# Two modulation tiles moved from a feed-forward's middle to beside the output projection ahead of it, and a rounding of value weights moved behind an exponential

## The chip, the core and the metric

The kernel runs on one core of a Trainium2 chip. The metric is the device time of one execution in microseconds. Before the change the median of three runs is 1470.91 us (1470.82 to 1471.57). One more execution was taken by the hardware profiler; it took 1470.03 us, and its trace, all of whose times count from the first instruction, spans 1468.2 us. Engine names: PE is TensorE (matmuls), DVE is VectorE, ACT is ScalarE, POOL is GpSimd, SP is the engine that issues most of the DMAs. Every engine works through its own instructions in order.

## The reference: what is computed

One step of a two-layer diffusion backbone for 128 context and 512 latent tokens of 1024 features:

```python
    for l in range(DEPTH):
        sh1_p, sc1_p, g1_p, sh2_p, sc2_p, g2_p = ada_modulation(cond_ctx, w_mod[l], b_mod[l])
        sh1_s, sc1_s, g1_s, sh2_s, sc2_s, g2_s = ada_modulation(cond_lat, w_mod[l], b_mod[l])
        hp = modulate(rms_norm(xp, norm_mix[l]), sh1_p, sc1_p)
        hs = modulate(rms_norm(xs, norm_mix[l]), sh1_s, sc1_s)
...
        xp = xp + g1_p * out_p
        xs = xs + g1_s * out_s
        hp = modulate(rms_norm(xp, norm_ffn[l]), sh2_p, sc2_p)
        hs = modulate(rms_norm(xs, norm_ffn[l]), sh2_s, sc2_s)
        xp = xp + g2_p * swiglu(hp, w_ffn_in[l], w_ffn_out[l])
        xs = xs + g2_s * swiglu(hs, w_ffn_in[l], w_ffn_out[l])
```

`ada_modulation` is silu(condition) @ w_mod + b_mod, 6 x 1024 numbers for each layer and condition. The mixer of layer 0 has 8 latent-attention (MLA) heads and 8 neighbourhood heads, that of layer 1 grouped-query attention. The feed-forward has 2816 hidden columns.

## The kernel before, in words

All 640 tokens stand along the free axis, the features along the 128 partitions. A float32 product is made of three matmuls of rounded parts (`mm3`: high x high, high x low, low x high). So each weight tile that comes from memory is split: ACT copies it to the rounded type (the high part, L175, L1490, L1025) and DVE subtracts that from the raw tile (the low part, L176, L1491, L1026).

**Modulation.** The sum over 1024 inputs for 128 modulation columns is one tile (`wm`, 128 x 1024 floats, 512 KB). For layer 0 part of it is made by PE (`mod0`: matmuls, a copy `modsb` by ACT at L373, a second small matmul, the bias by DVE at L381). The rest (layer 0's last gate, tiles 40 to 47 of `mods[0]`, and layer 1) is made by DVE: `one` (in `mod_side`) loads a tile and multiplies it with the broadcast conditions, once for each of the two conditions, summing as it goes (L1750, output `junk`). `mod_side` holds one list of 48 tiles in order and two functions that take from its front: `before` takes tiles beside an output projection (loads of L1768 into two buffers `ws`), as many after each of the 8 column blocks as a tuple says; `start` takes them inside the feed-forward, as many as `plan(kind, i)` says, for `kind` "fb" after hidden block i, for "n" in the feed-forward's output part.

**Neighbourhood heads** (layer 0) run from a written order of pieces for each head; the pieces of the values (`tail`) of one head run within the next. Beside head 6 the value weights of MLA (`wmv`, two halves of 128 x 512) are loaded and split at L1025 and L1026, well ahead of their use. `nexps[h, j]` is the instruction of head h's exponential j (L804), and `after(inst, fn)` has `fn`'s instructions issued behind `inst`. Other names there: `nts` are transposed probabilities split at L405 (ACT) and L409 (DVE), `no` the values' products, `ns` scores, `L475` and `L420` sum two halves of an output on DVE.

**Output projection of layer 0** (`mixer_out`, names `oa`): 8 column blocks; for each, weights `oaw` are split, PE multiplies, DVE adds gate x product to the residual stream (L335), ACT squares it (L213, L208) and DVE sums the squares (L214). Blocks 5 to 7 do their first token half first; `oanp` then sums over partitions on PE, and from its result come the feed-forward's inputs `h01`.

**Feed-forward of layer 0** (`ffn(0, ...)`). From hidden block 3 on, each block of 128 hidden columns is made by seven products instead of eight (a Strassen-like scheme) whose weights `wX`, `wW`, `wY`, `wZ` come out of `seven`: DVE adds the raw gate weights `rg` (`wg_`) and up weights `ru` (`wu_`) at L1298, L1299, L1302 and L1303 (output `s`), and ACT and DVE split them. The raw gate weights go into two buffers (`wr`), loaded at L1611. Per block PE does `fg<-..11`, `fd<-..D`, the last product `E` of the block before, `fg<-..N`, `fu`, `fd<-..22`, and `fg<-..C`, which may write its bank only when ACT has copied `u` from it (L1624). After the block's `E`, DVE multiplies gate and up (`sg`, L1599), ACT and DVE split the result (`hd`, L1550, L1551), and SP writes it out (`sp_`, L1556). A scheduler then places these instructions on each engine, by its own estimate of when they can run. As it has placed them, DVE makes the sums `s` of block N while PE is at the products of block N - 2, and the tile that the plan gives to block N, both products of it, runs on DVE in that same stretch. I call the stretch in which `s` of block N is made round N.

Of the kernel before, what the change touches and what calls it, by code (L numbers as in the profile page):

```python
# [13 lines left out]
AF = mybir.ActivationFunctionType  # L14
# [37 lines left out]
def body(ctx, tc, xT, vecs, crow, wm0, wm0g1, wm0g, wm1, wA, wNV, wNA, wMK, wMV, wOA, wGQ, wGK, wGV, wOC,  # L52
# [3 lines left out]
    V, S, G = nc.vector, nc.scalar, nc.gpsimd  # L56
# [32 lines left out]
    def bank(name, kind="m"):  # L89
        if kind == "m":  # L90
            return psp.tile([P, 512], F32, tag="m", bufs=4, name=name)
        return ypool["pool"].tile([P, 512], F32, tag=kind, bufs=ypool["tags"][kind], name=name)
# [13 lines left out]
    def f(ap):  # L106
        return ap.bitcast(F32)
# [13 lines left out]
    def sequence(order, pieces):  # L121

        left = dict(pieces)
        run([left.pop(name) for name in order.split() if name in left])
        assert not left, list(left)

    def named(prefix, pieces):
        return {f"{prefix}{i}": piece for i, piece in enumerate(pieces)}
# [17 lines left out]
    mods = [main.tile([P, 48, 2], F32, name=f"mods{l}") for l in range(2)]  # L146
# [32 lines left out]
    def after(inst, fn):  # L179
        if inst is None:  # L180
            return fn()
        with tc.issue_after(inst.ins):
            return fn()
# [340 lines left out]
    x = []  # L524
# [182 lines left out]
    nqk, wnas, done_with, nexps = {}, {}, {}, {}  # L707
# [242 lines left out]
    mqs, exps = {}, {}  # L950
# [24 lines left out]
    for h in range(8):  # L975
        p, r = divmod(h, 2)
        if r == 0:
            oN.append(ring.tile([P, T], F32, tag="x", name=f"oN{p}"))
            pfirst, psecond = prompt_pair([nv[4][:, 2 * p + i, :] for i in range(2)], oN[p], ab, f"npp{p}",
                                         lambda name: bank(name, "y"))  # L980
        pts = []
        sc = na_scores(h, bm, pts)
        if h < 7:
            bm = na_bias(h + 1)
        qh, ql, ks = [t[r] for t in nqk[p]]
        pieces = named("s", sc)
        if h in SPLIT_AT:
            pieces["pk"] = lambda h=h: after(nexps[h, 1], SPLIT_AT[h])

        def prompt_scores(pss, qh=qh, ql=ql, ks=ks):  # L990
            PE.matmul(pss, qh[:, NS:T], ks[:, 896:1024], start=True, stop=False)
            PE.matmul(pss, ql[:, NS:T], ks[:, 896:1024], start=False, stop=True)
        pieces["sp"] = pfirst(r, prompt_scores)
        if p < 3:
            pieces.update(named("q", na_q(p + 1) if r == 0 else na_k(p + 1)))
        for n, at in enumerate(M_AT):
            if h == at:
                pieces.update(named("n" if "m0" in pieces else "m", mod0(4 + n, lambda n=n: bank(f"mod{4 + n}", "y"),
                                                                               mod_raw_w if h == 6 else mod_raw)))
        if h == 7:  # L1000
            pieces.update(k_pieces(0, ybank))
            pieces.update(named("u", q_pieces(0, ybank, lambda c: ring.tile([P, T], F32R, tag="h" + c, name=f"mq{c}0"),
                                              lambda: f(tq[0]))))
        sequence(NA_ORDER[h] if h else "q0 q1 s0 m0 q2 s1 sp pk q3 q4 q5 m1 q6 q7 m2", {**pieces, **tail})
        tail = na_values(h, pts, oN[p])
        if r == 1:
            tail.update(psecond)
        if h == 6:
            mla_w(0)
            kT = [[ring.tile([P, T], F32R, tag="h" + c, name=f"kT{c}{r}") for r in range(2)] for c in "hl"]  # L1010
            kTp = ring.tile([P, T], F32R, tag="x", name="kTp")
            even_keys, first_odd = [[(kT[i][r], kTp[:, P * (2 * i + r):P * (2 * i + r + 1)]) for i in range(2)] for r in range(2)]
            odd_keys = [first_odd]
            wmvr = [ring.tile([P, T], F32R, tag="hh", name=f"wmvr{u}") for u in range(2)]
            tq = [ring.tile([P, T], F32R, tag="hh", name=f"tq{r}") for r in range(2)]
            with tc.issue_after(fetched["wm0r"].ins):
                for u in range(2):
                    fetched["wmvr"] = nc.sync.dma_start(f(wmvr[u][:, :512]), wMV[:, 512 * u:512 * u + 512])
                lat = latents()
            with tc.issue_after(fetched["near"].ins):  # L1020
                fetched["tq"] = nc.sync.dma_start(f(tq[0]), tabM[:, 0, :])
            wmv = wp.tile([P, 2, 1024], F32R, tag="w", bufs=3, name="wmv")
            for u in range(2):
                c = slice(512 * u, 512 * u + 512)
                S.activation(wmv[:, 0, c], f(wmvr[u][:, :512]), AF.Copy)  # L1025
                V.tensor_tensor(wmv[:, 1, c], f(wmvr[u][:, :512]), f(wmv[:, 0, c]), ALU.subtract)  # L1026
            wmv = wmv[:, 0, :], wmv[:, 1, :]
        if h == 7:
            with tc.issue_after(fetched["tq"].ins):
                for r in range(2):  # L1030
                    k_rope(r, (slice(64, 128), slice(0, 64))[r])
                nc.sync.dma_start(f(tq[1]), tabM[:, 1, :])
# [83 lines left out]
    tail, oM, oNs = {}, [], []  # L1116
# [33 lines left out]
    oMs = [after(exps[7, 3], lambda: rsplit(oM[p], f"oMs{p}")) for p in range(3)]  # L1150
# [639 lines left out]
    def x_again(n):  # L1790
# [5 lines left out]
    op = ffn_open(0)  # L1796
    box, nxt = next_mod("h01", gs[0][1], mods[0], SH2, op[7])
    side, before = mod_side([(0, wm0g, G2)] + [(1, wm1[j:j + 8], j) for j in (SH1, SC1, G1, SH2, SC2)],
                            lambda kind, i: int(4 < i < 20 and (i % 3 > 0 or i in (9, 15))) if kind == "fb" else
                            (0, 1, 1, 1, 2, 2, 2, 2, 3, 3, 3, 3, 3, 2, 2, 2)[i])  # L1800
    x, pend = mixer_out(wOA, oMs + oNs, [4, 5, 6, 7, 0, 1, 2, 3], x_again, mods[0], "oa", nxt, op[-1], before(op[1], op[5], (1, 1, 1, 1, 0, 0, 0)), True, hold=exps[7, 3])
    box2, nxt = next_mod("h10", gs[1][0], mods[1], SH1)
    x, pend = ffn(0, x, pend, box["m"], nxt, side, op)

# [187 lines left out]
    for h in range(8):  # L1992
# [4 lines left out]
        if h < 7:  # L1997
# [10 lines left out]
    op = ffn_open(1)  # L2008
    box, nxt = next_mod("h11", gs[1][1], mods[1], SH2, op[7])
    _, before = mod_side([(1, wm1[G2:], G2)], None)  # L2010
    x, pend = mixer_out(wOC, oGs, list(range(8)), lambda n, x=x: x[n], mods[1], "oc", nxt, op[-1],
                        before(op[5], op[5], (2, 1, 1, 2, 1, 1, 0)), True, hold=gexp[7, 3])
# [11 lines left out]
    x, pend = ffn(1, x, pend, box["m"], final, lambda pool: lambda kind, i: None, op)  # L2024
# [158 lines left out]
```

## Time and profile before

| What | us |
|---|---|
| median of 3 runs | 1470.91 |
| the profiled execution | 1470.03 |
| its span, first to last instruction | 1468.2 |
| neighbourhood head 6's end, where `wmv` is split | 187 to 202 |
| output projection `oa` of layer 0 | 311 to 369 |
| feed-forward of layer 0, seven-product blocks | 413 to 651 |
| its output part | 651 to 806 |
| product of a modulation tile and one condition on DVE (L1750) | 1.22 |
| load of a 512 KB tile `wm`, median from issue to landing | 4.4 |

A row of a timeline gives the start, the length, the engine, the line, the operation with its output and inputs, and in brackets how long the engine sat idle ahead of it and what ended that. Times of lists of waits are totals, counts and the longest.

### The profile page before, as it was taken

To read this page: it belongs to the slowest core of one execution; us is meant where nothing else is said; L and a number is where in the kernel's file an instruction comes from. 1 tells how busy PE (TensorE), PEld (TensorE's weight loads), DVE (VectorE), ACT (ScalarE), POOL (GpSimd) and SP (SyncE) were. 2 spreads that over 40 slices of the span, in tenths; PEclk is the share of its full clock that TensorE was granted. 3 is DMA by queue.
4 is the path that set the end of the run, shared out by engine and by line. 5 is a ranking of instruction groups with operands and counts; after the bars stand their busy time and mean duration, and the time that the engine had idled before them with its cause. 6 is when DMAs were issued, how large, how long until landed. Compare 5 with 4: busy or idle time off the path is not lost.

```text
span 1468.2 us, 25868 instructions
## 1 busy us (share of the span) xinstructions
PE 1435.2 (98%) x9764; PEld 1387.6 (95%) x9764; DVE 1230.0 (84%) x2353; ACT 776.6 (53%) x1531; POOL 179.4 (12%) x276
## 2 busy tenths in 40 slices
PE   5999999999999999999999999999999999999997
PEld 3989989899999999999999999989999999999997
DVE  5877778977998898856998888888899898989976
ACT  5446667853755454531223666672656555555443
POOL 0047635520000000000000122220000000000000
PEclk9999999999999999999999999999999999999999
DMA  9643460134265454468765200115245555548572
GB/s 370 223 155 125 145 188 17 44 136 138 89 214 179 159 167 156 161 231 319 228 224 158 98 30 30 57 50 170 84 167 196 178 181 178 178 141 293 185 268 72
DMA packets 82725, 234.18 MB, mean 160 GB/s; under 512 B 9256, under 2 KB 15560, under 8 KB 82216
## 3 DMA queue, kind: packets, MB, share of 16 engines
q1 hardware_dynamic: 80240, 228.12, 46.3%
q10 hardware_dynamic: 1944, 3.48, 0.7%
q8 instruction: 76, 1.25, 0.3%
q0 software_dynamic: 416, 0.93, 0.2%
q14 instruction: 49, 0.40, 0.1%
HBM read 192.82 MB, written 36.66 MB: 156 GB/s over the span
## 4 chain that ended last, share of the span: by engine, by line
PE 81%; DVE 9%; DMA 4%; ACT 3%; issue 2%; SPq 0%; DVEq 0%; ACTq 0%
PE fg L64 17%; PE fd L64 7%; PE fgo L64 5%; PE fo L64 5%; PE gq L64 3%; PE fu L64 3%; PE fdo L64 2%; PE nk L64 2%; PE go L64 2%; PE gs L64 2%; PE nq L64 1%; PE fuo L64 1%; PE gt L68 1%; DVE junk L1750 1%; PE mod L64 1%
## 5 line engine op out<-in xcount | busy, mean ns | idle before, releaser
L1750 DVE SCALAR_TENSOR_TENSOR junk<-wm,cb 128x1024 bf16<-128x1024 f32 x88 | 107.4, 1221 | 2.7 <-DMA wm<-in_wm 1.7
L64 PE MATMUL gq<-h10h,wgq 128*128 128x320 f32 x256 | 65.8, 316 | 0.0
L269 POOL TENSOR_SCALAR h10h<-h10t,gs,mods 128x320 fp32r<-128x320 f32 x4 | 3.9, 991 | 432.8 <-DVE h10t L263 426.8
L1490 ACT ACTIVATE wY<-s 128x1024 fp32r<-128x1024 f32 x38 | 40.3, 1061 | 23.3 <-PE fg L64 19.1
L2018 POOL TENSOR_TENSOR xr<-xw,fn1rs 128x320 f32<-128x320 f32 x2 | 1.7, 861 | 412.8 <-ACT fn1rs L237 412.8
L1599 DVE TENSOR_TENSOR sg<-up,sg 128x640 f32<-128x640 f32 x38 | 31.3, 824 | 21.5 <-ACT sg L1598 20.4
L1491 DVE TENSOR_TENSOR wZ<-s,wZ 128x1024 fp32r<-128x1024 f32 x38 | 46.4, 1220 | 1.3
L1490 ACT ACTIVATE wZ<-s 128x1024 fp32r<-128x1024 f32 x38 | 40.1, 1055 | 13.7 <-PE fd L64 9.0
L1491 DVE TENSOR_TENSOR wY<-s,wY 128x1024 fp32r<-128x1024 f32 x38 | 46.3, 1220 | 0.3
L64 PEld LDWEIGHTS gq<-h10h,wgq 128*128 128x128 f32 x256 | 44.9, 189 | 0.6
L1598 ACT ACTIVATE sg<-fg 128x320 f32<-128x320 f32 x38 | 16.7, 438 | 48.2 <-PE fg L64 48.2
L64 PE MATMUL fg<-h01C,wY 128*128 128x320 f32 x228 | 37.1, 311 | 2.7 <-ACT u L1624 2.7
L64 PE MATMUL gq<-h10l,wgq 128*128 128x320 f32 x128 | 39.4, 308 | 0.0
L1955 ACT ACTIVATE gp<-gs,gb,rq 128x640 f32<-128x640 f32 (+1 forms) x40 | 31.8, 796 | 13.2 <-DVE gb L1954 11.8
L1620 ACT ACTIVATE p<-fd 128x320 f32<-128x320 f32 x38 | 16.6, 437 | 40.7 <-PE fd L64 40.7
L64 PEld LDWEIGHTS fg<-h01C,wY 128*128 128x128 f32 x228 | 34.0, 188 | 4.2 <-ACT u L1624 4.2
L64 PE MATMUL fg<-h11N,wZ 128*128 128x320 f32 x228 | 36.7, 309 | 0.0
L64 PE MATMUL fg<-h01q,wX 128*128 128x320 f32 x228 | 36.7, 309 | 0.0
L64 PE MATMUL fu<-h11q,wX 128*128 128x320 f32 x228 | 36.6, 309 | 0.0
L64 PE MATMUL fg<-h01E,wW 128*128 128x320 f32 x228 | 36.6, 309 | 0.0
L64 PE MATMUL fg<-h01N,wZ 128*128 128x320 f32 x228 | 36.6, 309 | 0.0
L64 PE MATMUL fd<-h11q,wZ 128*128 128x320 f32 x228 | 36.6, 309 | 0.0
(3412 smaller groups left out, 5287.0 us busy)
## 6 DMA issues: line engine op xcount, KB each, us to landing
wm<-in_wm SPq DMA_DIRECT2D x48, 512.0 KB, 4.4
mraw<-in_wm SPq DMA_DIRECT2D x8, 1024.0 KB, 13.2
mraw<-in_wm SPq DMA_DIRECT2D x14, 512.0 KB, 3.8
wmv<-in_wm0g SPq DMA_DIRECT2D x8, 512.0 KB, 4.1
wm<-in_wm0g SPq DMA_DIRECT2D x8, 512.0 KB, 4.6
ruo<-in_wFO SPq DMA_DIRECT2D x8, 512.0 KB, 4.4
rgo<-in_wFO SPq DMA_DIRECT2D x8, 512.0 KB, 6.3
x<-in_xT SPq DMA_DIRECT2D x8, 320.0 KB, 5.7
```

The costliest lines, as they stand in the source:

```text
L64: cls.last = nc.tensor.matmul(*a, **k)
L68: cls.last = nc.tensor.transpose(*a, **k)
L269: G.tensor_scalar(h[:, c0:c1], t, self.gsl[:, k, 0:1], self.ml[:, self.sh + k, 0:1], ALU.mult, ALU.add)
L1490: S.activation(h, src, AF.Copy)
L1491: V.tensor_tensor(w_, src, f(h), ALU.subtract)
L1598: last = S.activation(sg[:, 0:HT], g[:, :HT], AF.Silu, scale=-1.0)
L1599: V.tensor_tensor(sg, up, sg, ALU.mult)
L1620: S.activation(p5, b5[:, :HT], AF.Copy)
L1750: V.scalar_tensor_tensor(junk, raw, 1.0, cb[:, c, :], ALU.mult, ALU.mult, accum_out=mods[l][:, j0 + i, c:c + 1])
L1955: gexp[h, j] = S.activation(dst, src, AF.Exp, bias=nb, scale=rq[:, j:j + 1], accum_out=ll[:, j:j + 1])
L2018: G.tensor_tensor(x[k][:, c0:c1], root[1][k], nrm.rs[:, c0:c1], ALU.mult)
```

## The change

Three edits. The tuple for the output projection of layer 0 gives six tiles instead of four (tiles 44 and 45 of `mods[0]`, after its blocks 5 and 6). The plan of the feed-forward no longer takes a tile at hidden blocks 9 and 15; every tile behind 45 is taken from the same list, so it comes at an earlier block than before; behind the blocks all is as it was. And the first half of `wmv`'s high part is issued behind the last exponential of head 6.

```diff
             for u in range(2):
                 c = slice(512 * u, 512 * u + 512)
-                S.activation(wmv[:, 0, c], f(wmvr[u][:, :512]), AF.Copy)
+                after(nexps[6, 3], lambda: S.activation(wmv[:, 0, c], f(wmvr[u][:, :512]), AF.Copy))
                 V.tensor_tensor(wmv[:, 1, c], f(wmvr[u][:, :512]), f(wmv[:, 0, c]), ALU.subtract)
...
     side, before = mod_side([(0, wm0g, G2)] + [(1, wm1[j:j + 8], j) for j in (SH1, SC1, G1, SH2, SC2)],
-                            lambda kind, i: int(4 < i < 20 and (i % 3 > 0 or i in (9, 15))) if kind == "fb" else
+                            lambda kind, i: int(4 < i < 20 and i % 3 > 0) if kind == "fb" else
                             (0, 1, 1, 1, 2, 2, 2, 2, 3, 3, 3, 3, 3, 2, 2, 2)[i])
-    x, pend = mixer_out(wOA, oMs + oNs, [4, 5, 6, 7, 0, 1, 2, 3], x_again, mods[0], "oa", nxt, op[-1], before(op[1], op[5], (1, 1, 1, 1, 0, 0, 0)), True, hold=exps[7, 3])
+    x, pend = mixer_out(wOA, oMs + oNs, [4, 5, 6, 7, 0, 1, 2, 3], x_again, mods[0], "oa", nxt, op[-1], before(op[1], op[5], (1, 1, 1, 1, 1, 1, 0)), True, hold=exps[7, 3])
```

What it moves. ACT at the end of head 6, as a difference of the two orders (`np` are head 6's exponentials, `modsb` the modulation's copy that PE waits for):

```order
 L175 ACTIVATE wm_2497<-wm0r 128x768
-L1025 ACTIVATE wmv<-wmvr_2505 128x512
 L405 ACTIVATE nts_2h<-nt_2_2436 128x512
 L804 ACTIVATE np_2_2408,nl_2350<-np_2_2408,nm_2349 128x384
 L804 ACTIVATE np_3_2414,nl_2350<-np_3_2414,nm_2349 128x384
 L373 ACTIVATE modsb_2466<-mod_2420 128x256
+L1025 ACTIVATE wmv<-wmvr_2505 128x512
 L448 ACTIVATE npp3p,npp3l_2450<-npp3s_2445,npp3m_2448 128x128
 L1025 ACTIVATE wmv<-wmvr_2506 128x512
```

The first copy moves behind two exponentials and `modsb`; the second stays. On DVE both bias additions of L381 then stand ahead of the second L1026, where one and then the other stood behind it.

DVE in the output projection, from the residual of block 4 on; before:

```order
L335 SCALAR_TENSOR_TENSOR xr_4534<-oa4a,mods_98,xr_4534 128x320
L176 TENSOR_TENSOR oaw_4610<-oaw6r,oaw_4610 128x1024
L214 TENSOR_TENSOR oanacc<-oanacc,oansq_4538 128x320
L335 SCALAR_TENSOR_TENSOR xr_4534<-oa4b,mods_98,xr_4534 128x192
L335 SCALAR_TENSOR_TENSOR xr_4534<-oa4b,mods_98,xr_4534 128x128
L176 TENSOR_TENSOR oaw_4648<-oaw7r,oaw_4648 128x1024
```

and after:

```order
L335 SCALAR_TENSOR_TENSOR xr_4534<-oa4a,mods_98,xr_4534 128x320
L1750 SCALAR_TENSOR_TENSOR junk_4577,mods_98<-wm_44_4575,cbo 128x1024
L214 TENSOR_TENSOR oanacc<-oanacc,oansq_4538 128x320
L1750 SCALAR_TENSOR_TENSOR junk_4579,mods_98<-wm_44_4575,cbo 128x1024
L335 SCALAR_TENSOR_TENSOR xr_4534<-oa4b,mods_98,xr_4534 128x192
L335 SCALAR_TENSOR_TENSOR xr_4534<-oa4b,mods_98,xr_4534 128x128
L176 TENSOR_TENSOR oaw_4616<-oaw6r,oaw_4616 128x1024
L214 TENSOR_TENSOR oanacc<-oanacc,oansq_4567 128x320
L1750 SCALAR_TENSOR_TENSOR junk_4621,mods_98<-wm_45_4619,cbo 128x1024
L176 TENSOR_TENSOR oaw_4660<-oaw7r,oaw_4660 128x1024
```

The rounding of the last two blocks' weights now stands behind products of tiles 44 and 45; the second product of 45 comes two rows further down, ahead of the feed-forward's first weights.

DVE in the feed-forward in round 9 (`sg_6` is the gated product of block 6); before:

```order
L1298 TENSOR_TENSOR s_9_6109<-wg_9r 128x512
L1491 TENSOR_TENSOR wY_8_5976<-s_8_5973,wY_8_5976 128x1024
L1299 TENSOR_TENSOR s_9_6109<-wu_9r,wg_9r 128x512
L1750 SCALAR_TENSOR_TENSOR junk_6314,mods_98<-wm_47_6312,cb 128x1024
L1302 TENSOR_TENSOR s_9_6115<-s_9_6109,wg_9r 128x512
L1750 SCALAR_TENSOR_TENSOR junk_6316,mods_98<-wm_47_6312,cb 128x1024
L1599 TENSOR_TENSOR sg_6_5723<-up_6_5722,sg_6_5723 128x640
```

and after:

```order
L1298 TENSOR_TENSOR s_9_6122<-wg_9r 128x512
L1491 TENSOR_TENSOR wY_8_5988<-s_8_5985,wY_8_5988 128x1024
L1299 TENSOR_TENSOR s_9_6122<-wu_9r,wg_9r 128x512
L1302 TENSOR_TENSOR s_9_6128<-s_9_6122,wg_9r 128x512
L1303 TENSOR_TENSOR s_9_6128<-s_9_6128,wu_9r 128x512
L1599 TENSOR_TENSOR sg_6_5735<-up_6_5734,sg_6_5735 128x640
```

The two products are gone from ahead of `sg`. On SP the load of the next gate weights (`wg_10r`) now stands ahead of the write of block 6's hidden tile instead of behind it. Round 15 changes in the same way.

## The prediction

> **What bounds the kernel now.** I read the page first, then PE's waits, then PE's own timeline, and last the engines that PE waits for. The page:
>
> ```profile
> span 1468.2 us, 25868 instructions
> PE 1435.2 (98%) x9764; PEld 1387.6 (95%) x9764; DVE 1230.0 (84%) x2353; ACT 776.6 (53%) x1531; POOL 179.4 (12%) x276
> ```
>
> TensorE (PE) is the bound, so a change on other engines can only win what PE loses in waits. In the list of PE's waits (total, times, longest) the largest beyond the start-up is this one:
>
> ```profile
> PE fg L64 <- ACT u L1624: 2.7, 5, 0.8
> ```
>
> It lies in the first feed-forward's middle. There PE runs seven products for each block of 128 hidden columns, and the seventh, `fg<-h01C`, must wait until ACT has copied the fifth's result out of the same bank (`u`). PE's timeline (start, length, what, idle time before it) has one such row in each round (round N: DVE prepares the weights of block N); for rounds 8 to 12, 15 to 17 and 19:
>
> ```profile
> 458.22 1.92 PE L64 MATMUL fg<-h01C,wY 128*128 128x320 f32 x12
> ...
> 470.92 2.02 PE L64 MATMUL fg<-h01C,wY 128*128 128x320 f32 x12 [0.23 <-ACT u L1624]
> ...
> 484.31 2.03 PE L64 MATMUL fg<-h01C,wY 128*128 128x320 f32 x12 [0.81 <-ACT u L1624]
> ...
> 497.67 2.03 PE L64 MATMUL fg<-h01C,wY 128*128 128x320 f32 x12 [0.78 <-ACT u L1624]
> ...
> 510.10 1.92 PE L64 MATMUL fg<-h01C,wY 128*128 128x320 f32 x12
> ...
> 547.03 1.92 PE L64 MATMUL fg<-h01C,wY 128*128 128x320 f32 x12
> ...
> 560.14 2.02 PE L64 MATMUL fg<-h01C,wY 128*128 128x320 f32 x12 [0.63 <-ACT u L1624]
> ...
> 572.93 2.03 PE L64 MATMUL fg<-h01C,wY 128*128 128x320 f32 x12 [0.22 <-ACT u L1624]
> ...
> 597.86 1.92 PE L64 MATMUL fg<-h01C,wY 128*128 128x320 f32 x12
> ```
>
> Undisturbed, a round takes (547.03 - 510.10) / 3 = 12.31 us. From round 8 to 19 there are 11 periods, 135.4 us at that pace, and they took 139.64: PE loses **4.2 us** here. The five idle times add up to only 2.67. I use the starts, because a row's end runs past the start of the next (12 matmuls are recorded as 1.92 long where they follow each other in a seventh of 12.31, 1.76), so each idle time is shown about 0.16 too short, and the smaller waits between rounds 17 and 19 aren't listed at all. The Trainium skill (Perfetto Trace Analysis, the section on the Tensor Engine's instruction) says that a matmul's end is computed, not observed, which agrees; by the idle times the sum below would be 1.5 us smaller.
>
> Why ACT is late: a loop between DVE, ACT, SP and DMA that is longer than PE's period. Rows of DVE, ACT and SP in round 9:
>
> ```profile
> 463.71 0.69 DVE L1298 TENSOR_TENSOR s<-wg_9r 128x512 f32<-128x512 f32 x1 [1.64 <-DMA wg_9r<-in_wFI]
> ...
> 466.05 1.22 DVE L1750 SCALAR_TENSOR_TENSOR junk<-wm,cb 128x1024 bf16<-128x1024 f32 x1
> ...
> 467.80 1.22 DVE L1750 SCALAR_TENSOR_TENSOR junk<-wm,cb 128x1024 bf16<-128x1024 f32 x1
> ...
> 468.94 0.82 DVE L1599 TENSOR_TENSOR sg<-up,sg 128x640 f32<-128x640 f32 x1
> 469.80 0.74 ACT L1550 ACTIVATE hd_0h<-sg 128x640 fp32r<-128x640 f32 x1 [3.39 <-DVE sg L1599]
> 470.94 0.43 SPq L1611 DMA_DIRECT2D wg_10r<-in_wFI  x1
> 477.10 0.69 DVE L1298 TENSOR_TENSOR s<-wg_10r 128x512 f32<-128x512 f32 x1 [1.84 <-DMA wg_10r<-in_wFI]
> ```
>
> `sg` is late because the two products of a modulation tile (`junk`) stand before it; the next weights are asked for behind `sg` (7.23 us after the loop began), and DVE then idles until they land. Round: 477.10 - 463.71 = 13.39, 1.08 over PE's 12.31. PE's `C` product of this round started 470.92 - 463.71 = 7.21 behind `s`. Round 12, without a tile:
>
> ```profile
> 503.58 0.69 DVE L1298 TENSOR_TENSOR s<-wg_12r 128x512 f32<-128x512 f32 x1 [1.66 <-DMA wg_12r<-in_wFI]
> 508.83 0.33 SPq L1611 DMA_DIRECT2D wg_13r<-in_wFI  x1
> 513.36 0.68 DVE L1298 TENSOR_TENSOR s<-wg_13r 128x512 f32<-128x512 f32 x1
> ```
>
> The weights are asked for after 5.25 us, DVE doesn't wait for them, and the round is 9.78. Five tiles in a row drive PE into waits; one round without a tile resets the loop.
>
> **The change, part by part.** *Tiles out of rounds 9 and 15.* The rounds with tiles become 7, 8 | 10, 11 | 13, 14 | 16, 17. Up to round 8 nothing differs in kind, and the `C` of round 8 shows no wait. Round 9 begins at 463.71 as before; without its two products (468.94 - 467.80 = 1.14 each) its `C` isn't waited for and starts at 458.22 + 12.31 = 470.53. Round 10's `s` comes at 463.71 + 9.78 = 473.5, or 3.26 behind the last `C` (513.36 - 510.10), 473.8, whichever is later. Its `C` could start at 473.8 + 7.21 = 481.0 and PE gets there at 482.84. Round 11: 473.8 + 13.39 + 7.21 = 494.4 against 495.15. Round 12 has no tile, and 13 and 14 start from a reset loop like 10 and 11, as do 16 and 17: 0.7 us is the smallest margin. Gain: all **4.2**. Its lower bound has the tile-free round as slow in its load as the others (wg_10r: 477.10 - 470.94 = 6.16 instead of 4.53, round 11.4). Three rounds are then 2 x 13.39 + 11.4 = 38.2 against PE's 36.9. The walk gives `C` starts 0.6, 0.2, 1.1, 0.2 and 1.1 us late in rounds 11, 13, 14, 16 and 17, 3.1 in all before rounding, and a gain of 1.1.
>
> *The same work beside the output projection.* Four products more on DVE, and two loads on SP: wm_44 ahead of oaw7r, wm_45 ahead of the feed-forward's first weights. PE waits nowhere in this stage. DVE between 343 and 358 us (busy), the landing times of all `wm` loads, and the rows that set the deadlines:
>
> ```profile
> 343.00:358.00 15.00, 9.40 (x15) 1.00 0.54 176
> DMA to landing us min/median/max: 3.3/4.4/7.2
> 335.12 1.22 DVE L1750 SCALAR_TENSOR_TENSOR junk<-wm,cbo 128x1024 bf16<-128x1024 f32 x1
> ...
> 343.29 0.54 DVE L335 SCALAR_TENSOR_TENSOR xr<-oa4a,mods,xr 128x320 f32<-128x320 f32 x1
> 343.75 1.21 DVE L176 TENSOR_TENSOR oaw<-oaw6r,oaw 128x1024 fp32r<-128x1024 f32 x1
> 344.89 0.48 DVE L214 TENSOR_TENSOR oanacc<-oanacc,oansq 128x320 f32<-128x320 f32 x1
> 346.77 0.68 DVE L335 SCALAR_TENSOR_TENSOR xr<-oa4b,mods,xr 128x192 f32<-128x192 f32 x2 [1.40 <-PE oa4b L64]
> ...
> 357.33 0.55 DVE L335 SCALAR_TENSOR_TENSOR xr<-oa,mods,xr 128x320 f32<-128x320 f32 x1 [1.89 <-PE oa L64]
> 350.09 0.31 PE L64 MATMUL oa6a<-oNs0h,oaw 128*128 128x320 f32 x1
> 359.77 0.70 PE L64 MATMUL oanp<-oanacc,ones 128*128 128x320 f32 x2
> ```
>
> 4 x 1.22 = 4.9 us go into 5.6 us of idle time, ahead of the last residual at 357.33, which waits for PE anyway; behind it 1.9 us remain until `oanp` needs the sums of squares. By the new order DVE starts wm_44's first product at 343.75, where rounding oaw6r's weights (`L176`) stood, and does that rounding behind the residual of 346.77: 346.77 + 0.68 + 1.21, near 348.7. PE wants them at 350.09. wm_44 can be asked for when wm_42's second product ends (336.3); with 7.2 us, the longest landing, it is there at 343.5. Cost: **0**.
>
> *The rounding of the value weights.* Rows of ACT, PE and DVE at the end of neighbourhood head 6:
>
> ```profile
> 192.89 0.63 ACT L1025 ACTIVATE wmv<-wmvr 128x512 fp32r<-128x512 f32 x1 [0.63 <-DMA wmvr<-in_wMV]
> 193.42 0.58 ACT L405 ACTIVATE nts_2h<-nt 128x512 fp32r<-128x512 f32 x1
> ...
> 195.10 0.37 ACT L373 ACTIVATE modsb<-mod 128x256 f32<-128x256 f32 x1
> 195.52 0.61 PE L64 MATMUL mod<-sel,modsb 128*128 128x4 f32 x4 [0.73 <-ACT modsb L373]
> 198.10 0.41 PE L64 MATMUL ns<-nk,nqh 128*128 128x384 f32 x1 [0.35 <-DVE mods L381]
> 201.54 0.50 PE L64 MATMUL no<-nts_0l,nv 128*128 128x512 f32 x1 [0.36 <-DVE nts_0l L409]
> 196.37 0.83 DVE L1026 TENSOR_TENSOR wmv<-wmvr,wmv 128x512 fp32r<-128x512 f32 x1 [0.36 <-DMA cq1l<-cqr]
> 197.20 0.57 DVE L475 TENSOR_TENSOR oN<-npp2o,npp2h 64x128 f32<-64x128 f32 x2
> ```
>
> With the first half's copy behind `modsb`, ACT no longer idles 0.63 for its load and the 0.53 of the copy is gone from ahead of `modsb`: it comes about 1 us earlier and the 0.73 goes. DVE's `L381` now stands ahead of the second `L1026`, so the 0.35 goes. What is late next is the third wait: DVE's chain `L475` to `L409` starts behind the second `L1026`, whose copy ACT ends about 0.4 earlier, and DVE saves the `L381` between. I put the chain 0.6 earlier; PE, 1.1 earlier before it, waits longer there. Gain: **0.6**. Ends: all three waits gone, 1.44; or the copy's 0.53 pushed onto the chain behind it, a loss.
>
> *Sum* against the profiled execution (1470.03, of which 1468.2 is span): 4.2 + 0 + 0.6 = 4.8, so 1465.2. The median of the runs is 0.88 above it: 1470.91 - 4.8 = **1466.1**.
>
> **The rivals.** A, *one empty round isn't enough*: the tile-free load takes as long as the rest. For it: wg_9r, wg_10r and wg_12r all landed too late for DVE (1.64, 1.84 and 1.66 idle), and round 12 was reached with PE 2.6 us behind its pace, which eased it. Against: in round 12, where the load was asked for without products ahead of it, it was hidden. Gain 1.1 + 0.6: 1469.2.
>
> B, *slower: wm_44 lands late*. DVE takes its work in order, so oaw6r's rounding stands behind wm_44's first product and the matmuls at 350.09 behind that. From that product's start to the rounding's end it is 1.22 + 0.48 + 1.22 + 0.68 + 1.21 = 4.8 us by the rows (at most, since DVE's rows overlap a little), so it decides from a start at 345.3, a landing of 9.0 us. PE then stops for each us more; slower by over 0.2% needs 4.8 + 2.9 = 7.7 more, a landing of nearly 17 us: 1473.8. Against it: the longest of these loads took 7.2. The Trainium skill (DMA: Bandwidth & Descriptors, section on queues, rings and completion order) has one queue's transfers consumed in ring order on each engine, which speaks for it; no run here shows that order.
>
> C, *nothing changes*: PE comes 4.8 earlier to the second half of the feed-forward and waits there for reloaded hidden tiles or weights instead: 1470.9. Against: PE shows no wait of 0.2 from 600 to 800 us, and those loads follow PE's own progress.
>
> The change does do what it says: both moves stand in the order.
>
> **How the numbers follow.** Forecast 0.65, A 0.20, B 0.05, C 0.10. Low end: all of 4.2 and 1.44 gone, 1465.3, less 0.3 for the runs' scatter: 1465.0. High end: 1.1 and nothing from the rounding, 1469.8; C and B lie outside. 0.2% is 2.9 us, about what can be told from no change here. Faster: the forecast and a part of A, 0.68; same: the rest of A and C, and a little of the forecast, 0.26; slower 0.06.
>
> **What would show it.** In the changed profile: `fg<-h01C` rows 12.31 apart from round 8 to 19 with no idle time; no PE wait in 343 to 372 us; wg_10r and wg_16r asked for about 5.3 behind their `s`; `modsb` not waited for, and a longer wait at `nts_0l`. Wrong if those rows still wait in rounds 11, 14 or 17 (A), if `oa6a` or `oanp` waits (B), or if they run smoothly and new waits appear behind 600 us (C).

## The result, and the profile after

The changed kernel takes 1466.43 us (median of 7 runs, 1465.12 to 1469.15) against 1471.29 (7 runs of before beside it): ratio 0.9967, 95% interval 0.9955 to 0.9979. That is 4.86 us faster, 3.1 to 6.6 by the interval. The forecast was 4.8, to 1466.1. Its profiled execution took 1467.04, with a span of 1465.3 (before: 1470.03 and 1468.2), so the two traces differ by only 2.9; the parts below add up to that and say what belongs to the change.

PE's timeline of the changed kernel at the seventh products of rounds 8 to 11, 16 and 19:

```profile
458.57 1.92 PE L64 MATMUL fg<-h01C,wY 128*128 128x320 f32 x12
470.88 1.92 PE L64 MATMUL fg<-h01C,wY 128*128 128x320 f32 x12
483.20 1.92 PE L64 MATMUL fg<-h01C,wY 128*128 128x320 f32 x12
495.50 1.92 PE L64 MATMUL fg<-h01C,wY 128*128 128x320 f32 x12
...
557.08 1.92 PE L64 MATMUL fg<-h01C,wY 128*128 128x320 f32 x12
...
594.01 1.92 PE L64 MATMUL fg<-h01C,wY 128*128 128x320 f32 x12
```

No row carries an idle time, and the eleven periods take 594.01 - 458.57 = 135.44 instead of 139.64: 4.20 less, every wait gone. The loop behind it, in rows of DVE and SP:

```profile
463.83 0.69 DVE L1298 TENSOR_TENSOR s<-wg_9r 128x512 f32<-128x512 f32 x1 [1.97 <-DMA wg_9r<-in_wFI]
469.08 0.33 SPq L1611 DMA_DIRECT2D wg_10r<-in_wFI  x1
474.03 0.69 DVE L1298 TENSOR_TENSOR s<-wg_10r 128x512 f32<-128x512 f32 x1 [0.24 <-DVE g L1630]
...
487.18 0.69 DVE L1298 TENSOR_TENSOR s<-wg_11r 128x512 f32<-128x512 f32 x1 [1.06 <-DMA wg_11r<-in_wFI]
500.80 0.69 DVE L1298 TENSOR_TENSOR s<-wg_12r 128x512 f32<-128x512 f32 x1 [2.15 <-DMA wg_12r<-in_wFI]
```

Round 9, now without a tile, asks for the next weights 469.08 - 463.83 = 5.25 us behind its beginning, and DVE finds them there when it comes. The rounds take 10.20, 13.15 and 13.62: 36.97 for three, where PE needs 36.93. The next two groups of three take 36.17 and 36.52 (`s` of blocks 15 and 18 starts at 536.97 and 573.49). So the loop is about as long as PE's period, with little over; the experiments show what that means.

At the end of neighbourhood head 6 (rows of ACT and PE of the changed kernel):

```profile
193.43 1.07 PE L64 MATMUL mod<-mraww,scol 128*32 128x256 f32 x16
195.05 0.37 ACT L373 ACTIVATE modsb<-mod 128x256 f32<-128x256 f32 x1
195.61 0.56 PE L64 MATMUL mod<-sel,modsb 128*128 128x4 f32 x4
200.94 0.50 PE L64 MATMUL no<-nts_0h,nv 128*128 128x512 f32 x1 [0.31 <-ACT nts_0h L405]
202.02 0.51 PE L64 MATMUL no<-nts_0l,nv 128*128 128x512 f32 x1 [0.58 <-DVE nts_0l L409]
```

The waits for `modsb` and for DVE's bias sum are gone, and the third has grown from 0.36 to 0.31 + 0.58. From the `mod<-mraww` product to the last row it is 8.59 us. In the trace of before that product's row is

```profile
192.45 1.07 PE L64 MATMUL mod<-mraww,scol 128*32 128x256 f32 x16
```

and the distance 201.54 - 192.45 = 9.09. Gain 0.50.

Beside the output projection (DVE and PE):

```profile
344.24 1.22 DVE L1750 SCALAR_TENSOR_TENSOR junk<-wm,cbo 128x1024 bf16<-128x1024 f32 x1
...
347.85 1.21 DVE L176 TENSOR_TENSOR oaw<-oaw6r,oaw 128x1024 fp32r<-128x1024 f32 x1
350.57 0.31 PE L64 MATMUL oa6a<-oNs0h,oaw 128*128 128x320 f32 x1
...
357.82 0.55 DVE L335 SCALAR_TENSOR_TENSOR xr<-oa,mods,xr 128x320 f32<-128x320 f32 x1 [0.94 <-PE oa L64]
```

oaw6r's rounding ends at 349.06, 1.5 ahead of its matmuls, and DVE still waits for PE at the last residual. PE waits nowhere here.

One wait is new. At the end of the feed-forward's output part, where the sums of squares for the next norm (`fn0acc`, DVE) go into PE's `fn0p`, PE waits 1.0. SP, DVE, ACT and PE in the trace after:

```profile
701.49 0.33 SPq L1661 DMA_DIRECT2D wo_01r<-in_wFO  x1
701.84 1.08 DVE L1667 TENSOR_TENSOR wo<-wo_00r,wo 128x896 fp32r<-128x896 f32 x1
707.61 0.85 ACT L1666 ACTIVATE wo<-wo_01r 128x768 fp32r<-128x768 f32 x1 [5.90 <-DMA wo_01r<-in_wFO]
794.52 0.78 PE L64 MATMUL fn0p<-fn0acc,ones 128*128 128x320 f32 x2 [1.01 <-DVE fn0acc L214]
```

and in that of before:

```profile
705.35 0.33 SPq L1661 DMA_DIRECT2D wo_01r<-in_wFO  x1
705.70 1.08 DVE L1667 TENSOR_TENSOR wo<-wo_00r,wo 128x896 fp32r<-128x896 f32 x1
710.72 0.85 ACT L1666 ACTIVATE wo<-wo_01r 128x768 fp32r<-128x768 f32 x1 [5.21 <-DMA wo_01r<-in_wFO]
796.06 0.49 DVE L214 TENSOR_TENSOR fn0acc<-fn0acc,fn0sq 128x320 f32<-128x320 f32 x1 [0.54 <-ACT fn0sq L213]
797.21 0.70 PE L64 MATMUL fn0p<-fn0acc,ones 128*128 128x320 f32 x2
```

From round 23's seventh product (647.11 before, 643.26 after) to this row it is 150.10 before and 151.26 after: 1.16 more. DVE's last sum ended 796.06 + 0.49 = 796.55 before, 0.66 ahead of PE. Its work from 651 to 794 us is a sequence in which it rounds output weights and multiplies tiles; in it stands a load of output weights (`wo_01r`) that took 6.1 us from issue to use after, and 5.4 before. Up to this load DVE hasn't fallen behind PE: its rounding of `wo_00r`, the load ahead, starts 701.84 - 643.26 = 58.58 us behind round 23's seventh product after, and 705.70 - 647.11 = 58.59 before. So DVE has come 4 us earlier together with PE, and the lateness begins at `wo_01r`.

Sum of the two traces: 0.50 + 4.20 - 1.16 = 3.5 gained by these three. The start-up was 1.0 slower in the trace after (the first selection product of the modulation starts at 20.07, before at 19.07), ahead of all that the change touches. What is left, 0.4, is spread over differences of 0.1 to 0.2.

### The profile page after: what moved, and what is told of

Its sections match the earlier page's. It is cut to its first block, busy times and chain, and to the rows that moved or that the text cites. A ratio compares the mean times of both kernels' runs of the same rounds, so it can differ in the third digit from the quotient of the medians.

```text
span 1465.3 us, 25865 instructions
## 1 busy us (share of the span) xinstructions
PE 1436.0 (98%) x9764; PEld 1388.0 (95%) x9764; DVE 1232.1 (84%) x2353; ACT 778.9 (53%) x1531; POOL 178.7 (12%) x276
## 4 chain that ended last, share of the span: by engine, by line
PE 83%; DVE 9%; ACT 3%; issue 3%; DMA 2%; DVEq 0%; ACTq 0%
PE fg L64 21%; PE fd L64 9%; PE fgo L64 5%; PE fu L64 5%; PE gq L64 3%; PE fdo L64 2%; DVE junk L1750 2%; PE fo L64 2%; PE nk L64 2%; PE go L64 2%; PE gs L64 2%; PE nq L64 1%; PE fuo L64 1%; PE mod L64 1%; PE gt L68 1%
## 5 line engine op out<-in xcount | busy, mean ns | idle before, releaser
L1750 DVE SCALAR_TENSOR_TENSOR junk<-wm,cb 128x1024 bf16<-128x1024 f32 x84 | 102.4, 1219 | 1.9 <-DMA wm<-in_wm 0.9
L1750 DVE SCALAR_TENSOR_TENSOR junk<-wm,cbo 128x1024 bf16<-128x1024 f32 x28 | 34.1, 1218 | 6.9 <-DMA wm<-in_wm 3.8
L64 PE MATMUL fd<-h01q,wZ 128*128 128x320 f32 x228 | 36.6, 309 | 0.0
L64 PE MATMUL fg<-h11q,wX 128*128 128x320 f32 x228 | 36.5, 309 | 0.0
```

The lines of the kernel that those rows point to most:

```text
L64: cls.last = nc.tensor.matmul(*a, **k)
L1750: V.scalar_tensor_tensor(junk, raw, 1.0, cb[:, c, :], ALU.mult, ALU.mult, accum_out=mods[l][:, j0 + i, c:c + 1])
```

## The experiments

Theory: the rounds are limited by a loop (request, landing, tile, next request) that is longer than PE's period, and one round without a tile after every two resets it. Rivals: only the number of tiles counts; the tile's load holds up the weights, not its products; the copy brings the gain. Second question: is the wait at `fn0p` the price of an earlier PE, and can it be had back?

All medians and ratios, and three stretches of PE's timeline in each profile (starts of rows as above): N is `mod<-mraww` to `nts_0l` of head 6's end, M rounds 8 to 19 of the middle, O round 23 to `fn0p`.

| Kernel | median us | ratio to before, 95% | N | M | O |
|---|---|---|---|---|---|
| before | 1471.29 | | 9.09 | 139.64 | 150.10 |
| changed | 1466.43 | 0.9967 (0.9955 to 0.9979) | 8.59 | 135.44 | 151.26 |
| copy alone | 1471.22 | 1.0001 (0.9992 to 1.0010) | 8.61 | 139.27 | 150.09 |
| tiles alone | 1467.31 | 0.9967 (0.9954 to 0.9979) | 8.96 | 136.14 | 151.08 |
| changed, second time | 1466.12 | 0.9962 (0.9950 to 0.9975) | 8.61 | 136.00 | 150.47 |
| changed, third time | 1466.54 | 0.9962 (0.9949 to 0.9974) | 8.61 | 135.44 | 150.09 |
| one tile moved | 1468.63 | 0.9980 (0.9971 to 0.9988) | 9.12 | 137.54 | 150.09 |
| three rounds in a row | 1469.66 | 0.9985 (0.9976 to 0.9994) | 8.60 | 139.85 | 150.09 |
| no loads | 1467.29 | 0.9966 (0.9954 to 0.9978) | 8.94 | 135.63 | 150.09 |
| no products | 1467.81 | 0.9971 (0.9960 to 0.9981) | 8.37 | 136.91 | 150.09 |
| late rounds used | 1467.65 | 0.9968 (0.9956 to 0.9981) | 8.61 | 137.20 | 150.09 |
| four tiles moved | 1466.73 | 0.9966 (0.9953 to 0.9978) | 8.61 | 135.46 | 150.11 |
| output part earlier | 1468.65 | 0.9976 (0.9966 to 0.9985) | 8.60 | 136.12 | 152.46 |
| the same, nine tiles | 1470.84 | 0.9989 (0.9980 to 0.9998) | 8.60 | 135.44 | 153.88 |

The runs of before beside them had medians of 1471.43 (copy alone, tiles alone, second time, one tile), 1471.88 (three in a row, no loads, no products, late rounds) and 1472.39 (the rest).

**Copy alone.** Of the diff only the line at L1025:

```diff
-                S.activation(wmv[:, 0, c], f(wmvr[u][:, :512]), AF.Copy)
+                after(nexps[6, 3], lambda: S.activation(wmv[:, 0, c], f(wmvr[u][:, :512]), AF.Copy))
```

> Only the rounding of the value weights is moved; all twelve tiles stay in the feed-forward's rounds. By the theory (three waits at the end of neighbourhood head 6, of which two go and the third grows) PE gains 0.5 there and nothing elsewhere: about 1470.8 against 1471.3, not to be told from no change by the time alone. In its trace no wait at the selection product for modsb, and at nts_0h and nts_0l together 0.9 instead of 0.4. Rival: the copy behind the last exponential only moves the lateness on to the next head and nothing is won: 1471.3, with waits at nts_0h and nts_0l that sum to 1.4 or more.

The time can't be told from before's. The trace shows the expected 0.5: N is 8.61, with the same two waits as in the changed kernel. What the new order really does shows across the table: with the copy behind the exponential N is 8.59 to 8.61 in all nine profiles; with the old order it is 8.94 to 9.12 in four and 8.37 in the fifth ("no products", which changes nothing at this place). In the four ACT sat idle 0.45 to 0.65 ahead of its copy, until `wmvr` landed. In the fifth it had no idle time there, so `wmvr` had landed already:

```profile
192.60 0.63 ACT L1025 ACTIVATE wmv<-wmvr 128x512 fp32r<-128x512 f32 x1
```

So the old order is 0.2 better when the load is in time and 0.3 to 0.5 worse when it isn't; the change takes the load out of the path. Mean of the five old ones 8.90: a gain of 0.3, too small for the times.

**Tiles alone.** The two other edits of the diff, with L1025 as before.

> Only the two tiles are moved; the value weights are rounded as before. The loop theory: no wait at the seventh products and 135.4 us from round 8 to round 19 instead of 139.6, a gain of 4.2 up to the end of the middle. If DVE then sets the end of the first feed-forward's output (theory of the giving back) PE waits there about 1 us for fn0acc, and the whole gains 3.0 to 3.3 (1468.1); if that wait was a chance of one execution, the whole gains 4.2 (1467.1). Rival, that the time of the changed kernel comes mostly from the copy: under 1 us here.

Ratio 0.9967, as the changed kernel: the gain is the tiles'. M is 136.14, 3.5 less than before and 0.7 more than in the changed kernel: the loss begins behind the weights `wg_12r`, used 7.43 us after their request, where 6.16 was reckoned with. The wait at `fn0p` is there again (0.84).

**The changed kernel again**, twice, with its file unchanged.

> The changed kernel once more, for a second profile of it. The middle takes 135.4 from round 8 to 19 again. If the wait of 1.0 at fn0p belongs to the order (DVE's work in the output stage is too long for a PE that comes earlier), it is there again, 0.7 to 1.3; if it comes from two loads that happened to land late (wo_01r and wo_51r), it is under 0.3 here and the span is 1 us shorter at that place. Time 1466 to 1468.

> The changed kernel a third time, beside the other three on the same chip. 1466 to 1467, the middle at 135.4 to 136.2, and a wait at fn0p of 0.2 to 1.1.

O is 150.47 and 150.09. The third execution, rows of SP, ACT and PE:

```profile
701.50 0.33 SPq L1661 DMA_DIRECT2D wo_01r<-in_wFO  x1
706.11 0.85 ACT L1666 ACTIVATE wo<-wo_01r 128x768 fp32r<-128x768 f32 x1 [3.31 <-DMA wo_01r<-in_wFO]
793.35 0.70 PE L64 MATMUL fn0p<-fn0acc,ones 128*128 128x320 f32 x2
```

The same load, issued at the same time, is used 4.6 us later instead of 6.1, and there is no wait at `fn0p`, where 0.2 to 1.1 was expected. In the three profiles with such a wait (0.2 to 1.0) `wo_01r` took 5.9 to 6.2. `wo_51r`, the other load that the expectation names, was used 5.3 us after its request in the first execution and 3.5 in the other two. So the wait goes with late loads, the second side of the expectation: both late, 1.16; `wo_01r` alone, 0.38; neither, 0. (In tiles alone, 0.98 more than before, `wo_01r` took 5.9 and a third load, `wo_21r`, 4.7 where these three have 3.2 to 3.9.) An earlier PE doesn't bring it by itself, since the third execution and "four tiles moved" have a PE as early and no wait. Whether the loads come late more often behind an earlier PE is open (in before and in the copy alone `wo_01r` took 5.4 and 4.9), and why `wo_01r` takes 4.6 once and 6.1 another time isn't shown by these runs.

**One tile moved.** Against before, the tile of block 9 only:

```diff
-                            lambda kind, i: int(4 < i < 20 and (i % 3 > 0 or i in (9, 15))) if kind == "fb" else
+                            lambda kind, i: int(4 < i < 20 and (i % 3 > 0 or i == 15)) if kind == "fb" else
-    ... before(op[1], op[5], (1, 1, 1, 1, 0, 0, 0)) ...
+    ... before(op[1], op[5], (1, 1, 1, 1, 1, 0, 0)) ...
```

> Only one tile is moved, that of round 9, and one more stands beside the output projection (five); the tile of round 15 stays, so rounds 13 to 17 have five tiles in a row; the copy is as before. By the loop theory rounds 8 to 12 run at 12.31 and the gain there is 2.6; from round 15 to 19 the 1.6 that is lost now stays lost: idle rows of 0.6 and 0.2 at the seventh products of rounds 16 and 17. The whole about 2.6 better (1468.7), less what is given back at fn0p. Rival, that any lighter load of the rounds as a whole would do it (the number of tiles counts and not their spacing): half, 2.1, spread over both ends.

PE's seventh products in rounds 14 to 16 and 18 of this kernel:

```profile
533.39 1.92 PE L64 MATMUL fg<-h01C,wY 128*128 128x320 f32 x12
546.30 2.03 PE L64 MATMUL fg<-h01C,wY 128*128 128x320 f32 x12 [0.44 <-ACT u L1624]
559.15 2.02 PE L64 MATMUL fg<-h01C,wY 128*128 128x320 f32 x12 [0.27 <-ACT u L1624]
...
584.60 2.03 PE L64 MATMUL fg<-h01C,wY 128*128 128x320 f32 x12 [0.45 <-ACT u L1624]
```

Up to round 14 (533.39) the period is 12.31; from there, with tiles in rounds 13 to 17 without a gap, 2.1 is lost, where 1.6 in rounds 16 and 17 was expected. The gain lies where the empty round is, as the loop has it; the whole is 2.8 better by the medians, forecast 2.6.

**Three rounds in a row.** The changed kernel with its ten tiles grouped otherwise:

```diff
-                            lambda kind, i: int(4 < i < 20 and i % 3 > 0) if kind == "fb" else
+                            lambda kind, i: int(i in (5, 7, 8, 9, 11, 12, 13, 15, 16, 17)) if kind == "fb" else
```

> The changed kernel, with its ten tiles of the rounds grouped otherwise: 5, then 7 to 9, 11 to 13, 15 to 17, three in a row and then one round without. Nothing else differs. Loop theory: four rounds take 3 x 13.39 + 9.78 = 49.95 against PE's 49.24, so the third tile of each group makes the seventh product late: about 0.2 to 0.4 in round 9, 0.5 in round 13, 0.9 in round 17, 1.6 in all from round 8 to 19 (137.0 instead of 135.4). Since PE has about 1 us to wait at fn0p anyway, the whole is 0.5 to 1.6 slower than the changed kernel. Rival (only the number of tiles counts): no wait in these rounds, the time of the changed kernel.

PE's rows in rounds 8, 9, 13, 16 and 17 (the starts of the idle ones lie 0.6 to 1.0 late, and a little more is lost in the rounds behind them):

```profile
458.25 1.92 PE L64 MATMUL fg<-h01C,wY 128*128 128x320 f32 x12
471.38 2.05 PE L64 MATMUL fg<-h01C,wY 128*128 128x320 f32 x12 [0.66 <-ACT u L1624]
...
521.79 2.03 PE L64 MATMUL fg<-h01C,wY 128*128 128x320 f32 x12 [0.88 <-ACT u L1624]
...
560.03 2.02 PE L64 MATMUL fg<-h01C,wY 128*128 128x320 f32 x12 [0.74 <-ACT u L1624]
572.95 2.03 PE L64 MATMUL fg<-h01C,wY 128*128 128x320 f32 x12 [0.35 <-ACT u L1624]
```

M is 139.85: in this profile the same ten tiles in other rounds lose as much as the twelve in that of before. The waits stand where the loop puts them, at the third tile of each group (in the last group at the second already), but they are more than twice what I worked out (4.4 lost in M, forecast 1.6); DVE's rounds with a tile took 12.9 (round 16) to 15.1 (round 15) and not 13.39 each. That only the number counts is ruled out. But by the medians the kernel is still 2.2 faster than before, where the changed kernel is 4.9 to 5.9 faster, each against before beside it. The two profiles make the loss look larger than it is on the whole (this one took 1470.38, 0.7 above its median; that of before lies 1.3 below its own). So of the changed plan's gain about 3 us hang on the spacing. The copy's 0.3 and the smaller number of tiles may account for the other 2.2; these runs don't divide it.

**No loads** and **no products.** Both start from before. In the first the two tiles of rounds 9 and 15 aren't loaded, in the second all but 16 columns of their products are left out (such a product then takes 0.17):

```diff
-                    one(lambda src, name: load(src, D, name), box[0], fp)
+                    one((lambda src, name: box[0][:, 0, :]) if kind == "fb" and at in (9, 15) else
+                        lambda src, name: load(src, D, name), box[0], fp)
```

```diff
-        def one(raw_, cb, pool):
+        def one(raw_, cb, pool, w=D):
-                V.scalar_tensor_tensor(junk, raw, 1.0, cb[:, c, :], ALU.mult, ALU.mult,
+                V.scalar_tensor_tensor(junk[:, :w], raw[:, :w], 1.0, cb[:, c, :w], ALU.mult, ALU.mult,
-                    one(lambda src, name: load(src, D, name), box[0], fp)
+                    one(lambda src, name: load(src, D, name), box[0], fp, 16 if kind == "fb" and at in (9, 15) else D)
```

> The kernel before, but the tiles of rounds 9 and 15 aren't loaded: their products are made with the broadcast condition vector in the tile's place, so DVE's work is the same, 512 KB less is moved in each of the two rounds, and two columns blocks of the modulation are of other numbers. Theory that both halves of the loop's 13.39 count (7.23 up to the request, of which the two products are 2.0, and 6.16 for the load, which would be 4.5 without the tile beside it): round 9 takes about 11.8, rounds 8 to 19 lose 1 to 3 instead of 4.2. If only DVE's products count: 4.2 lost as before. If only the tile's load counts, by holding up the weights' load: nothing lost, 135.4 us.

> The kernel before, but of the tiles of rounds 9 and 15 only 16 of 1024 columns are multiplied (0.1 instead of 1.22 each); the tiles are loaded as before, so the DMA's work is the same; two blocks of modulation columns are sums over 16 entries only. Both halves count: the weights are asked for 5.3 behind the round's beginning and land 6.2 later, a round of 11.5, and rounds 8 to 19 lose 1 to 3 instead of 4.2. Only DVE's products count: nothing lost, 135.4 us. Only the load counts: 4.2 lost as before.

Without the loads M is 135.63, but the kernel doesn't tell what it was made for. Rows of DVE and SP at round 9:

```profile
459.92 1.22 DVE L1750 SCALAR_TENSOR_TENSOR junk<-cb 128x1024 bf16<-128x1024 f32 x1
465.67 0.69 DVE L1298 TENSOR_TENSOR s<-wg_9r 128x512 f32<-128x512 f32 x1
466.87 1.22 DVE L1750 SCALAR_TENSOR_TENSOR junk<-cb 128x1024 bf16<-128x1024 f32 x1
470.79 0.33 SPq L1611 DMA_DIRECT2D wg_10r<-in_wFI  x1
```

With no load to wait for, the scheduler has put one of the two products ahead of the round, and the request comes after 470.79 - 465.67 = 5.12 us, as in a round without a tile. Two things changed at once; inconclusive. Without the products, round 9 in DVE's and SP's rows:

```profile
463.95 0.69 DVE L1298 TENSOR_TENSOR s<-wg_9r 128x512 f32<-128x512 f32 x1 [1.70 <-DMA wg_9r<-in_wFI]
469.28 0.33 SPq L1611 DMA_DIRECT2D wg_10r<-in_wFI  x1
474.53 0.69 DVE L1298 TENSOR_TENSOR s<-wg_10r 128x512 f32<-128x512 f32 x1 [0.43 <-DMA wg_10r<-in_wFI]
...
569.72 0.42 SPq L1611 DMA_DIRECT2D wg_18r<-in_wFI  x1
577.62 0.69 DVE L1298 TENSOR_TENSOR s<-wg_18r 128x512 f32<-128x512 f32 x1 [3.67 <-DMA wg_18r<-in_wFI]
```

The tile is still loaded, and yet the request comes after 5.33, the weights are used 5.25 later and the round takes 10.58: nearly a round without a tile. It is 2.81 shorter than the 13.39 of before: 7.23 - 5.33 = 1.90 by the earlier request, 6.16 - 5.25 = 0.91 by a shorter landing. So the two products make a round long, for the most part by delaying the request, and the tile's load alone doesn't. Why the weights also land sooner, with the tile still loaded, isn't shown. M came out within the range of the theory that both halves count (1 to 3 lost), but not for its reason: the 1.5 that this kernel loses stands at round 18's seventh product (a wait of 1.10), behind a load of `wg_18r` that took 577.62 - 569.72 = 7.90.

**Late rounds used.** The changed kernel with two tiles out of the output part:

```diff
-                            lambda kind, i: int(4 < i < 20 and i % 3 > 0) if kind == "fb" else
-                            (0, 1, 1, 1, 2, 2, 2, 2, 3, 3, 3, 3, 3, 2, 2, 2)[i])
+                            lambda kind, i: int(4 < i < 22 and (i % 3 > 0 or i == 21)) if kind == "fb" else
+                            (0, 1, 1, 1, 2, 2, 2, 2, 3, 3, 2, 3, 2, 2, 2, 2)[i])
```

> The changed kernel, with two tiles more taken out of the feed-forward's output stage (one each from its eleventh and thirteenth step) and put into rounds 20 and 21 of the middle, where DVE has 3 to 5 us of idle time in a row. If DVE sets the end of the output stage, it is done there 4 x 1.22 = 4.9 us of work earlier at most, the wait of 1.0 for fn0acc goes and the whole is about 1.1 faster than the changed kernel, 1465.3. If the wait was a chance of late loads, no difference. Against: round 20 follows round 19 with a tile, and then 21, three in a row, and the loads of the output weights come behind two more tiles; if that hits PE, it shows as a wait at fo_0a or at the seventh product of round 21, up to 1 us slower.

The wait at `fn0p` is gone (O 150.09), though `wo_01r` took 6.1 here too. But the tile of block 21 was placed at rounds 20 and 21, not in the idle time behind them, and rounds 19 to 23 take 50.18 instead of 49.25; in M 1.8 is lost at waits in rounds 12 and 17, whose plan is the changed kernel's (the first behind `wg_12r`, used 7.41 us after its request). Nothing won: 1467.65.

**Four tiles moved.** The changed kernel with two tiles more beside the output projection:

```diff
-                            lambda kind, i: int(4 < i < 20 and i % 3 > 0) if kind == "fb" else
+                            lambda kind, i: int(4 < i < 17 and i % 3 > 0) if kind == "fb" else
-    ... before(op[1], op[5], (1, 1, 1, 1, 1, 1, 0)) ...
+    ... before(op[1], op[5], (1, 1, 1, 1, 2, 2, 0)) ...
```

> The changed kernel with two tiles more beside the output projection (two at each of the last two steps that have one) and none in rounds 17 and 19 of the middle. In the changed kernel's trace oaw6r's rounding ends 1.5 us before its matmul and oaw7r's about 2.4; four products of 1.22 more, two ahead of oaw6r's and two more ahead of oaw7r's, should make PE wait about 1 us at oa6a and 1.5 to 2 more at the last piece: slower than the changed kernel by about 2.5 us, 1469. Rival (the cover in this stage is larger than the idle time shown, since PE can run ahead elsewhere): the changed kernel's time. The rounds 17 to 19 without tiles give nothing, since nothing waited there.

The expectation fell: no loss that shows in the time (1466.73 beside 1466.54 for the changed kernel on the same chip), and PE's only wait in this stage is 0.34 at the second `oanp`. PE and DVE at the place:

```profile
349.93 1.22 DVE L176 TENSOR_TENSOR oaw<-oaw6r,oaw 128x1024 fp32r<-128x1024 f32 x1
349.97 0.31 PE L64 MATMUL oa6a<-oNs0h,oaw 128*128 128x320 f32 x1
...
350.26 0.31 PE L64 MATMUL oa<-oNs0h,oaw 128*128 128x320 f32 x1
...
350.56 0.31 PE L64 MATMUL oa5b<-oNs0h,oaw 128*128 128x320 f32 x1
...
351.29 0.33 PE L64 MATMUL oa6a<-oNs0h,oaw 128*128 128x320 f32 x1
```

oaw6r's rounding now runs from 349.93 to 351.15, but PE needs it only for the third matmul at 351.29. In between the scheduler has placed matmuls that don't need the low part, and pieces of the second token half (`oa5b`) that stand ready. Where a plan is made anew, idle time of DVE isn't the whole cover: PE's order moves too. A load that lands late in one execution is another matter, since no plan knows of it.

**Output part earlier**, and **the same with nine tiles** in the middle:

```diff
-                            (0, 1, 1, 1, 2, 2, 2, 2, 3, 3, 3, 3, 3, 2, 2, 2)[i])
+                            (1, 2, 1, 1, 2, 2, 2, 2, 3, 3, 2, 3, 2, 2, 2, 2)[i])
```

```diff
-                            lambda kind, i: int(4 < i < 20 and i % 3 > 0) if kind == "fb" else
-                            (0, 1, 1, 1, 2, 2, 2, 2, 3, 3, 3, 3, 3, 2, 2, 2)[i])
+                            lambda kind, i: int(4 < i < 20 and i % 3 > 0 and i != 14) if kind == "fb" else
+                            (2, 2, 1, 1, 2, 2, 2, 2, 3, 3, 2, 3, 2, 2, 2, 2)[i])
```

> The changed kernel with two tiles of the output stage moved from its eleventh and thirteenth step to its first and second, where DVE has idle times of 1 to 3 us. The middle is untouched. If DVE is what is late at fn0p, the wait there (0.2 to 1.0 in three profiles) goes and the whole is 0.4 to 1.2 faster than the changed kernel, about 1465.5. If the tiles' loads and products get in the way of the first output weights, PE waits at fo pieces near 660 to 690 us for wo weights, and nothing is won or up to 2 us lost.

> As the one before, and one tile more out of the middle (round 14's) to the first step of the output stage. Three profiles of the plan with ten tiles show the middle at 135.4, 136.1 and 136.0, so 0 to 0.7 is lost where a load is late; with round 14 free, rounds 13 to 15 have one tile in three and the loop has a margin of over 2 us there. Middle at 135.4 to 135.7; with the wait at fn0p gone as well the whole is 0.5 to 1.5 faster than the changed kernel, 1465.2. If the output stage's first step can't take a second tile, PE waits near 660 us instead.

Both are slower than the changed kernel beside them, by 2.1 and 4.3 us. The wait at `fn0p` is gone in both, but PE waits elsewhere, at 680 to 699 us; from the list of its waits (total, times, longest) in the second:

```profile
PE fo_4a L64 <- DVE wo L1667: 1.1, 1, 1.1
PE fo L64 <- DVE wo L1667: 0.9, 1, 0.9
PE fo_6a L64 <- DVE wo L1667: 0.9, 1, 0.9
```

The tiles that come earlier stand ahead of the rounding of the output weights on DVE, and PE waits for that. DVE's idle times there, which I had taken for room, lie ahead of roundings that PE needs soon. No version in this study beats the changed kernel.

## Why the prediction was right

- **The loop**: forecast 4.2 from the rounds, measured 4.20 in the profiled execution. The steps held: the request 5.25 behind `s` in the empty round (forecast 5.3), round 10's `s` at 474.03 (473.8), no wait in rounds 11, 14 and 17. The reading from starts is borne out as well: the five idle times listed before add up to 2.67, and 4.20 was won. The Trainium skill (Perfetto Trace Analysis, the section on the Tensor Engine's instruction) says that a matmul's end is computed, not observed, and this agrees: a gain read off the listed gaps would have been 1.5 too small. About 0.8 of that is the five gaps' 0.16 each; the rest is waits too short to be listed.
- **Its margin**: the walk goes by one trace's loads and leaves out how widely they spread. I gave 0.7 us as the smallest margin, in round 11. In the profiled execution it was 495.50 - 487.18 - 7.21 = 1.1 there, but one late load takes more. Six profiles have the changed plan's ten tiles in these rounds (changed three times, tiles alone, late rounds used, output part earlier): M is 135.44 twice, 136.00 to 136.14 three times and 137.20 once. Where it is longer, the loss begins behind gate weights that were asked for in a round with a tile and used 7.2 to 7.4 us later, not 6.16 (`wg_15r` 7.20 in the second execution, `wg_12r` 7.43 and 7.41, `wg_9r` 7.23). So 0.6 to 1.8 of the 4.2 was lost in four of six. This is not rival A: A has the load late that the tile-free round asks for, and DVE waited for none of those in the six. A fell.
- **Beside the output projection**: forecast 0, measured 0 (PE takes the same time to `oanp` within 0.05 in all profiles), by the order that was read. Rival B did not occur: wm_44's first product starts at 344.24, ahead of the 345.3 from which it would decide.
- **The value weights**: forecast 0.6, 0.50 in the trace, and 0.3 against the mean of the old order's five profiles. The `L475` to `L409` chain behind the second copy was late next, as said.
- **Rival C**: its sign was there, a new wait behind 600 us: 1.16, 0.38 and 0 in three executions of the same kernel. Its mechanism isn't shown. C has PE come too early for the loads of this part. But, as was argued against it, they follow PE: `wo_01r` is asked for 58.2 us behind round 23's seventh product in before and in all three, and in the traces of before and after DVE keeps the same distance up to `wo_00r`. What differs is how long single loads then took. I had looked for reloads from 600 to 800 and for PE's waits in that stretch, and not for how near DVE's sums of squares already were to PE there: before, `fn0acc`'s last sum ends 0.66 ahead of `fn0p`, in the copy alone 1.3.

Of the sum, 4.2 + 0 + 0.6, the traces confirm 4.2 + 0 + 0.5, less 0 to 1.2 in the output part and, in four of six profiles, 0.6 to 1.8 in the middle; the sum has neither of these two. By the medians the gain is 4.9, and 5.3 and 5.9 when measured again; the spans of the three profiled executions lie 2.9, 3.8 and 4.0 below that of before. The profiled execution of before lies 1.3 below the median of its runs, so typical executions of before lose more than its trace shows; where, is open. That the medians agree with 4.8 to within 0.1 is therefore partly luck: what the sum leaves out on one side is made up by what before's trace doesn't show on the other.

## What to carry to other kernels

When an engine waits a little in every round, look for a loop of request, landing and work on other engines and compare its length with the waiting engine's period. If it is longer (here by 1.08 in 12.31), the waits grow with the number of rounds in a row, and where the empty rounds stand counts, not only how many there are: here for about 3 of 5 us. Read the loss from the starts of the same instruction round by round, not from the idle times. And before a new wait is called the price of a gain, place the other engine against the same row of the bound engine in both traces, and profile the same kernel again: here DVE had moved along with PE, and 0.66 to 1.3 us of room stood against a load that varied by 1.6.

## What was not expected of the hardware

Loads spread widely with nothing changed in the program. `wo_01r` (128 x 768 floats, 384 KB), issued at 701.41 to 701.50 in three executions of the changed kernel, was first used 6.1, 6.2 and 4.6 us later, by an ACT that was waiting for it. The raw gate weights of a round (512 KB), where DVE waited for them, came 4.87 us (round 15) to 7.90 us (round 17) after the request in one and the same execution (no products). In a loop about as long as PE's period, such a late load goes with the loss of 0.6 to 1.8 us where there is one.
